# Twelve heads' softmax weights turned by VectorE and two DMAs in place of TensorE

## The chip, the cores and the metric

The kernel runs on one core of a Trainium2 chip. That core has a matrix engine (TensorE, PE in the profile; its weight loads are PEld), three engines for the rest (VectorE = DVE, ScalarE = ACT, GpSimd = POOL), a queue engine (SyncE = SP) and sixteen DMA engines that carry what any queue issues. The metric is the device time of one execution in microseconds (us), lower is better; times are given as the median of several runs.

## The reference

The reference is a two-layer encoder on 256 tokens of width 2048 in float32. A layer modulates and normalises `x`, projects it to the rows of two attention mixers and two gates, merges both mixers through their gates, projects back and adds; then a gated feed-forward part with a depthwise convolution follows. Mixer A has 8 heads over 2 groups of keys (a window of 128 tokens and a learned sink), mixer B has 8 heads over a 64-wide grid with a learned bias. For each head:

```python
s = jnp.einsum('bnqgrd,bnkgd->bgrnqk', qb, kw) * (HEAD_DIM ** -0.5)
p = jnp.exp(s - m)
p = p / (jnp.sum(p, axis=-1, keepdims=True) + jnp.exp(snk - m))
o = jnp.einsum('bgrnqk,bnkgd->bnqgrd', p, vw)
```

A head's `p` is a 256 x 256 matrix of softmax weights with queries in its rows. The product with the values sums over keys, so on this chip, which sums over partitions, `p` has to be turned first: keys into partitions.

## The kernel before

All large matrices come as one stream of weights per layer: units of 128 x 2048 float32 (1 MB), 232 to a layer, loaded by SP into four buffers `raw`. `unit_steps` (L280) makes two float32r halves of each half unit: ScalarE copies the upper part (L297) and VectorE subtracts it (L298), into four buffers `hl`. A half unit is named by its number here: 30.0 and 30.1 are the two halves of unit 30. TensorE takes three products from them (`feature_block`, L314 to L316, or `tokens`, L377 to L379). Modulation weights `aw` share the `raw` buffers and are reduced on VectorE (L226).

Small work runs beside that stream. After each unit `Paced.tick` (L258) first runs the functions that were deferred to this tick and then advances each job by its rate, in steps per unit. The attention of a layer is such a job (`attention`, L842): a step of the job advances every live head by one `yield` and starts at most one more. ATT gives the steps per unit while mixer A's rows arrive, ATT_B from the end of mixer A's projection on; what is left is run at once by `bg.finish(job)` (L952). In `attend` (L602) a head makes scores `sc` on TensorE (L607), masks and finds the maximum on VectorE (L610), takes exponentials and scales by the denominator on ScalarE (L618, L626), yields, turns `p` by four transposes on TensorE into the PSUM tile `tp` (L631), splits that into `pT` (L389 and L390, in `split`), yields, and multiplies with the values into `po` (L639), which becomes `oA` or `oB` (L641, L642).

The tile framework schedules each engine's queue from this program order, adds the waits, and each engine runs its own queue in order. SP issues all DMAs of this kernel. GpSimd does little here: among other things the power -0.5 for the norms of queries and keys (`rsqrt`, L441, tile `qrs`), for which VectorE then waits in `norm` (L556, tile `qn`). `packs` hold the rows of queries, keys and values; `qTa[:, i]` is head i's turned query in mixer A, `b[:, 8 + i]` and `b[:, i]` are query and key of a head in mixer B. In layer 1 (SCORES_3) a head first copies its query and key into float32r halves, so that those rows are free from then on.

Of the kernel before, what the change touches and what calls it, by code (L numbers as in the profile page):

```python
# [26 lines left out]
EPS = 1e-6  # L27
NEG = -1e30
SCALE = HEAD ** -0.5
GRID_W, NA_KH, NA_KW = 64, 8, 16  # L30


QKV_GROUPS = [1024, 0, 512, 2560, 3584, 1536, 3072, 4096, 2048]
# [44 lines left out]

H_RATE = [2.7, 1.7]

ATT = [1.288, 0.4]
ATT_B = [0.21, 0.21]

SCORES_3 = (1,)

ADA_ORDER = [[p * KC + k for k in range(KC) for p in ps] for ps in ((0, 1), (2,), (3, 4), (5,))]
ADA_ORDER = [i for part in ADA_ORDER for i in part]
# [47 lines left out]
def encoder(ctx: ExitStack, tc: tile.TileContext, a: dict, out: bass.AP):  # L135
# [16 lines left out]
    sm = pool("sm", 3)  # L152
    mm = pool("mm", 4, space=bass.MemoryType.PSUM)
    ax = pool("ax", 3, space=bass.MemoryType.PSUM)

    ident = const.tile([P, P], F32, name="ident")
    make_identity(nc, ident[:])
# [118 lines left out]
                pass  # L276

    bg = Paced()

    def unit_steps(l, u, by_halves=False):  # L280

        raw = rawp.tile([P, UB * P], F32, name=f"w{l}_{u}", tag="raw")
        if not by_halves:
            nc.sync.dma_start(raw[:], a["ws"][l, u])
        halves = []
        streamed = any(m == "w_in" and mo < GATE_A // P for m, _, mo in STREAMS[l][u * UB : (u + 1) * UB])
        at = OFF if streamed else 0
        for j in range(2):  # L290
            n = UB * P // 2
            hl = hlp.tile([P, 2 * n + ROW], F32R, name=f"hl{l}_{u}_{j}", tag="hl")
            hl = hl[:, at : at + 2 * n].rearrange("p (a n) -> p a n", a=2)
            r = raw[:, j * n : (j + 1) * n]
            if by_halves:
                nc.sync.dma_start(r, a["ws"][l, u][:, j * n : (j + 1) * n])
            nc.scalar.copy(hl[:, 0], r)  # L297
            nc.vector.tensor_tensor(out=hl[:, 1], in0=r, in1=hl[:, 0].bitcast(F32), op=ALU.subtract)  # L298
            halves.append(hl)
            if j == 0:  # L300
                yield halves
# [84 lines left out]
    def split(dst, src, scale=None):  # L386

        if scale is None:
            nc.scalar.copy(dst[:, 0], src)  # L389
            nc.vector.tensor_tensor(out=dst[:, 1], in0=src, in1=dst[:, 0].bitcast(F32), op=ALU.subtract)  # L390
            return
        nc.scalar.activation(out=dst[:, 0], in_=src, func=AF.Copy, scale=scale)
        nc.vector.scalar_tensor_tensor(
            out=dst[:, 1], in0=src, scalar=scale, in1=dst[:, 0].bitcast(F32), op0=ALU.mult, op1=ALU.subtract
        )
# [203 lines left out]

        return ((0, 0), (0, 1), (1, 0))[: 2 * len(x) - 1]  # L600

    def attend(q, k, v, p, mask, scale, sink, o):  # L602

        sc = ax.tile([P, 2, S], F32, name="sc", tag="ax")
        for t in range(2):
            for i, j in by(q):
                nc.tensor.matmul(sc[:, t], q[i][:, t * P : (t + 1) * P], k[j], start=i + j == 0, stop=(i, j) == by(q)[-1])  # L607
        m = sm.tile([P, 2], F32, name="m", tag="m")
        for t in range(2):
            nc.vector.tensor_tensor_reduce(  # L610
                out=p[:, t], in0=sc[:, t], in1=mask[:, t], scale=scale, scalar=-3.0e38 if sink is None else sink,
                op0=ALU.add, op1=ALU.max, accum_out=m[:, t : t + 1],
            )
        nm = sm.tile([P, 2], F32, name="nm", tag="nm")
        nc.vector.tensor_scalar(out=nm[:], in0=m[:], scalar1=-1.0, scalar2=None, op0=ALU.mult)
        den = sm.tile([P, 2], F32, name="den", tag="den")
        for t in range(2):
            nc.scalar.activation(out=p[:, t], in_=p[:, t], func=AF.Exp, bias=nm[:, t : t + 1], accum_out=den[:, t : t + 1])  # L618
        if sink is not None:
            es = sm.tile([P, 2], F32, name="es", tag="es")  # L620
            nc.scalar.activation(out=es[:], in_=nm[:], func=AF.Exp, bias=sink)
            nc.vector.tensor_tensor(out=den[:], in0=den[:], in1=es[:], op=ALU.add)
        ri = sm.tile([P, 2], F32, name="ri", tag="ri")
        nc.vector.reciprocal(out=ri[:], in_=den[:])
        for t in range(2):
            nc.scalar.activation(out=p[:, t], in_=p[:, t], func=AF.Copy, scale=ri[:, t : t + 1])  # L626
        yield
        tp = ax.tile([P, 2, S], F32, name="tp", tag="ax")
        for k in range(2):
            for t in range(2):  # L630
                nc.tensor.transpose(tp[:, k, t * P : (t + 1) * P], p[:, t, k * P : (k + 1) * P], ident[:])  # L631
        pT = at.tile([P, 2, 2, S], F32R, name="pT", tag="pT", bufs=1)
        split(pT, tp[:])
        v = v()
        yield
        po = ax.tile([P, 512], F32, name="po", tag="ax")
        for i, j in by(v):
            for b in range(2):
                nc.tensor.matmul(po[:, :S], v[i][:, b], pT[:, j, b], start=i + j + b == 0, stop=i + b == 2)  # L639
        o = o()  # L640
        nc.scalar.copy(o[:, 0], po[:, :S])  # L641
        nc.vector.tensor_tensor(out=o[:, 1], in0=po[:, :S], in1=o[:, 0].bitcast(F32), op=ALU.subtract)  # L642
# [115 lines left out]
    for l in range(L):  # L758
# [41 lines left out]
        def head_a(i):  # L800
            g = i // (HA // GA)
            if i >= 6:
                oA.append(paired(F32R, f"oA{l}_{i}"))
            elif i % 2 == 0:
                o = place(("y0", "y1", "y2")[i // 2], 4, F32R, f"oA{l}_{i}")
                oA.extend((o[:, :2], o[:, 2:]))
            q = in_halves(qTa[:, i], f"qA{l}_{i}", "qh", l in SCORES_3)
            if i % (HA // GA) == 0:
                kvs[0] = in_halves(kTa[:, g], f"kA{l}_{g}", "kh", l in SCORES_3)
            k = kvs[0]  # L810
            yield
            p = at.tile([P, 2, S], F32, name="p", tag="p")

            def v():
                if i % (HA // GA) == 0:
                    kvs[1] = in_halves(packs[0][:, 1:4:2, g * HEAD : (g + 1) * HEAD], f"vA{l}_{g}", "vh", True)
                return kvs[1]

            yield from attend(q, k, v, p, tables[0], SCALE, sink[:, i : i + 1], lambda: oA[i])

        def head_b(hb):
            b, i = packs[1 + hb // 4], hb % 4
            v = b[:, 4:8].rearrange("p (t a) s -> p t (a s)", t=2)
            p = at.tile([P, 2, S], F32, name="p", tag="p")
            nc.sync.dma_start(p[:], a["bias"][l, hb])
            q = in_halves(b[:, 8 + i], f"qB{l}_{hb}", "qh", l in SCORES_3)
            k = in_halves(b[:, i], f"kB{l}_{hb}", "kh", l in SCORES_3)
            yield
            yield from attend(
                q, k, lambda: in_halves(v[:, :, i * HEAD : (i + 1) * HEAD], f"vB{l}_{hb}", "vh", True), p, p, 1.0, None,  # L830
                lambda: oB_of(hb),
            )

        def oB_of(hb):
# [314 lines left out]
```

## Time and profile before

| What | us |
|---|---|
| Median of 3 runs | 2664.6 |
| Lowest and highest | 2664.26 and 2664.67 |
| Profiled execution: span from its first instruction to its last | 2663.2 |
| TensorE busy in it | 2650.9 |
| VectorE busy | 2102.2 |
| ScalarE busy | 1412.8 |
| GpSimd busy | 36.2 |

The page gives the profiled execution's time as its span; no other time of it is listed. The median of the runs stands 1.4 us above that span.

In the lines of the profile a group reads: source line, engine, operation, output tile <- input tiles, shapes, x count, then busy time, mean length in ns, and the idle time before with what ended it. A row of the timeline or of the chain of waits begins with its start and its length in us. A row of the view of waits reads: who waited, for whom, us in total, times, longest. A row of DMA issues ends with the KB of one and the median us from issue to landing.

### The profile page before, as it was taken

What the parts mean: (1) busy time and instruction counts of PE and PEld (TensorE: products, weight loads), DVE (VectorE), ACT (ScalarE), POOL (GpSimd) and SP (SyncE); (2) the same over time, 40 slices, a digit from 0 to 9 for tenths busy, and PEclk for the clock granted to TensorE, in tenths of its full rate; (3) what the DMA queues carried; (4) which work ended last, traced back from release to release, by engine and by line L of the source; (5) the groups of instructions that cost most, each with busy time, mean ns of one, the idle gap of its engine ahead of it and who ended that gap; (6) DMA issues with size and microseconds to landing.
All of it is one profiled execution on the core that took longest, in us unless ns stands there. A gap on an engine that the chain in (4) does not pass through costs nothing.

```text
span 2663.2 us, 50845 instructions
## 1 busy us (share of the span) xinstructions
PE 2650.9 (100%) x21256; PEld 2565.7 (96%) x21256; DVE 2102.2 (79%) x2959; ACT 1412.8 (53%) x2284; POOL 36.2 (1%) x25
## 2 busy tenths in 40 slices
PE   9999999999999999999999999999999999999999
PEld 7888899999999999999998889999999999999999
DVE  8898998997987888788976667768888866655664
ACT  5445865456644555355555566554565445544553
POOL 0001100000000000000000000000000000000000
PEclk9999999999999999999999999999999999999999
DMA  9987789885787878788766666666747765555554
GB/s 372 351 327 292 262 300 352 317 320 199 291 294 287 302 288 295 289 294 289 290 217 254 228 229 231 245 252 253 285 173 288 297 256 190 190 194 194 197 191 143
DMA packets 102039, 700.41 MB, mean 263 GB/s; under 512 B 12721, under 2 KB 15025, under 8 KB 17969
## 3 DMA queue, kind: packets, MB, share of 16 engines
q1 hardware_dynamic: 101810, 697.17, 71.4%
q8 instruction: 166, 2.72, 0.4%
q14 instruction: 63, 0.52, 0.1%
HBM read 695.03 MB, written 2.10 MB: 262 GB/s over the span
## 4 chain that ended last, share of the span: by engine, by line
PE 89%; DVE 6%; ACT 1%; issue 1%; DMA 1%; POOL 0%; SPq 0%; DVEq 0%; ACTq 0%
PE ps L314 25%; PE ps L316 25%; PE ps L315 25%; PE ps_t L377 4%; PE ps_t L379 4%; PE ps_t L378 4%; DVE hl L298 2%; DVE aw L226 2%; DMA aw<-in_aw 1%; PE sc L607 1%; PE po L639 1%; ACT hl L297 1%; PE tp L631 1%; POOL qrs L441 0%; PE qtp L580 0%
## 5 line engine op out<-in xcount | busy, mean ns | idle before, releaser
L298 DVE TENSOR_TENSOR hl<-w,hl 128x1024 fp32r<-128x1024 f32 x928 | 1128.3, 1222 | 360.0 <-ACT hl L297 357.6
L297 ACT CAST hl<-w 128x1024 fp32r<-128x1024 f32 x928 | 970.7, 1049 | 748.5 <-PE ps L316 518.1
L314 PE MATMUL ps<-h,hl 128*128 128x256 f32 x3328 | 922.8, 277 | 1.3 <-DVE ya L915 0.6
L315 PE MATMUL ps<-h,hl 128*128 128x256 f32 x3328 | 919.8, 276 | 0.0
L316 PE MATMUL ps<-h,hl 128*128 128x256 f32 x3328 | 919.8, 277 | 0.0
L314 PEld LDWEIGHTS ps<-h,hl 128*128 128x128 f32 x3328 | 624.8, 188 | 2.4 <-DVE ya L915 0.8
L315 PEld LDWEIGHTS ps<-h,hl 128*128 128x128 f32 x3328 | 625.3, 188 | 0.4 <-DVE h L470 0.2
L316 PEld LDWEIGHTS ps<-h,hl 128*128 128x128 f32 x3328 | 624.4, 188 | 0.0
L226 DVE CUSTOM_DVE_ANT_0 aw<-aw,cact,ab 128x2048 f32<-128x2048 f32 x189 | 443.5, 2347 | 48.8 <-DMA aw<-in_aw 47.8
L377 PE MATMUL ps_t<-hl,h 128*128 128x512 f32 x576 | 223.1, 392 | 2.6 <-ACT h L469 2.1
L378 PE MATMUL ps_t<-hl,h 128*128 128x512 f32 x576 | 224.9, 391 | 0.3
L379 PE MATMUL ps_t<-hl,h 128*128 128x512 f32 x576 | 224.3, 390 | 0.0
L994 DVE SCALAR_TENSOR_TENSOR u<-ps,cw,u 128x255 f32<-128x255 f32 x304 | 146.1, 481 | 66.5 <-ACT u L992 62.2
L992 ACT ACTIVATE u<-ps,cw 128x256 f32<-128x256 f32 x152 | 85.9, 565 | 187.9 <-PE ps L316 187.5
L316 PE MATMUL ps<-merged,hl 128*128 128x256 f32 x512 | 141.8, 277 | 0.4 <-DVE hl L298 0.4
L315 PE MATMUL ps<-merged,hl 128*128 128x256 f32 x512 | 141.6, 277 | 0.0
L314 PE MATMUL ps<-merged,hl 128*128 128x256 f32 x512 | 141.6, 277 | 0.0
L315 PE MATMUL ps<-act_o,hl 128*128 128x256 f32 x512 | 141.4, 276 | 0.0
L316 PE MATMUL ps<-act_o,hl 128*128 128x256 f32 x512 | 141.3, 276 | 0.0
L314 PE MATMUL ps<-act_o,hl 128*128 128x256 f32 x512 | 141.2, 276 | 0.0
L377 PEld LDWEIGHTS ps_t<-hl,h 128*128 128x128 f32 x576 | 107.9, 188 | 26.1 <-ACT h L469 3.1
L378 PEld LDWEIGHTS ps_t<-hl,h 128*128 128x128 f32 x576 | 108.1, 188 | 23.7 <-DVE hl L298 1.9
(231 smaller groups left out, 4612.5 us busy)
## 6 DMA issues: line engine op xcount, KB each, us to landing
w<-in_ws SPq DMA_DIRECT2D x463, 1024.0 KB, 4.9
aw<-in_aw SPq DMA_DIRECT2D x189, 1024.0 KB, 6.1
p<-in_bias SPq DMA_DIRECT2D x16, 256.0 KB, 4.2
x<-in_xT SPq DMA_DIRECT2D x4, 512.0 KB, 5.3
aw_o<-in_aw SPq DMA_DIRECT2D x2, 1024.0 KB, 12.3
out<-x SPq DMA_DIRECT2D x16, 128.0 KB, 2.1
w<-in_ws SPq DMA_DIRECT2D x2, 512.0 KB, 11.7
aw_b<-in_aw SPq DMA_DIRECT2D x1, 1024.0 KB, 18.1
```

The lines of the kernel that those rows point to most:

```text
L226: nc.vector.tensor_tensor_reduce(out=raw[:], in0=raw[:], in1=cact[:], scale=1.0, scalar=ab[:, i : i + 1], op0=ALU.mult, op1=ALU.add, accum ...
L297: nc.scalar.copy(hl[:, 0], r)
L298: nc.vector.tensor_tensor(out=hl[:, 1], in0=r, in1=hl[:, 0].bitcast(F32), op=ALU.subtract)
L314: nc.tensor.matmul(out, hi, act[0], start=first, stop=False)
L315: nc.tensor.matmul(ps[:, :S], hi, act[1], start=False, stop=False)
L316: nc.tensor.matmul(out, lo, act[0], start=False, stop=last)
L377: nc.tensor.matmul(ps[:], xh, hi, start=kc == kcs[0], stop=False)
L378: nc.tensor.matmul(ps[:], xh, lo, start=False, stop=False)
L379: nc.tensor.matmul(ps[:], xl, hi, start=False, stop=kc == kcs[-1])
L607: nc.tensor.matmul(sc[:, t], q[i][:, t * P : (t + 1) * P], k[j], start=i + j == 0, stop=(i, j) == by(q)[-1])
L992: nc.scalar.activation(out=u, in_=ps, func=AF.Identity, scale=w[:, 1:2], bias=w[:, 3:4])
L994: nc.vector.scalar_tensor_tensor(out=u[:, to], in0=ps[:, of], scalar=w[:, j : j + 1], in1=u[:, to], op0=ALU.mult, op1=ALU.add)
```

## The change

In layer 1 six heads of mixer A and six of mixer B (MOVED) no longer turn `p` on TensorE. VectorE transposes it in blocks of 32 x 32 into two rows that are free by then: for mixer A the head's own query row and a spare tile (two buffers, tag `r`), for mixer B the head's query and key rows. Eight DMAs on GpSimd's queue then write those blocks to their turned places in a DRAM tile `pY`, four for each row of blocks, each of 32 partitions in pieces of 32 elements (128 bytes). Two DMAs on SP's queue read the turned matrix back into the same two rows, and `pT` is split from there in two pieces of 128 x 256 in place of one of 128 x 512.

When the read-back is issued is fixed by `later`: three units (mixer A) or four (mixer B) after the head was turned, or when the head comes to need it. It carries a manual dependence on the last weight split on VectorE that had been made by then (`halved`). A moved head takes two more `yield`s. For layer 1 ATT goes from 0.4 to 0.42 and ATT_B from 0.21 to 0.32.

```diff
+BEHIND = mybir.DependencyInfo(mybir.DependencyClass.Sync, mybir.DependencyReason.DATA)
+BLOCK = 32
-ATT = [1.288, 0.4]
-ATT_B = [0.21, 0.21]
+ATT = [1.288, 0.42]
+ATT_B = [0.21, 0.32]
+BACK = [3, 4]
+MOVED = [(0, 0), (6, 6)]
...
+    dram = pool("dram", 2, space=bass.MemoryType.DRAM)
...
+    def later(n, fn):
+        if n == 0:
+            fn()
+        else:
+            bg.defer(lambda: later(n - 1, fn))
+
+    def turned_blocks(p, rows):
+        y = dram.tile([P, 2, S], F32, name="pY", tag="pY")
+        to = y[:].rearrange("(b i) k (t a j) -> t a i k b j", i=BLOCK, t=2, a=P // BLOCK)
+        for t, row in enumerate(rows):
+            nc.vector.transpose(out=row, in_=p[:, t])
+            src = row.rearrange("p (k b j) -> p k b j", k=2, j=BLOCK)
+            for a in range(P // BLOCK):
+                nc.gpsimd.dma_start(to[t, a], src[a * BLOCK : (a + 1) * BLOCK])
+        return y
...
-            nc.vector.tensor_tensor(out=hl[:, 1], in0=r, in1=hl[:, 0].bitcast(F32), op=ALU.subtract)
+            halved[0] = nc.vector.tensor_tensor(
+                out=hl[:, 1], in0=r, in1=hl[:, 0].bitcast(F32), op=ALU.subtract
+            ).ins.name
...
-    def attend(q, k, v, p, mask, scale, sink, o):
+    def attend(q, k, v, p, mask, scale, sink, o, rows=None):
...
+        if rows is not None:
+            rows = rows()
+            y = turned_blocks(p, rows)
+
+            def back():
+                for k in range(2):
+                    tc.add_manual_dep(nc.sync.dma_start(rows[k], y[:, k]).ins, halved[0], BEHIND)
+
+            back = once(back)
+            later(BACK[sink is None], back)
+            yield
+            yield
+            back()
+            pT = at.tile([P, 2, 2, S], F32R, name="pT", tag="pT", bufs=1)
+            for k in range(2):
+                split(pT[:, :, k], rows[k])
+        else:
+            tp = ax.tile([P, 2, S], F32, name="tp", tag="ax")
...
+            def rows():
+                spare = ev.tile([P, S], F32, name=f"spare{l}_{i}", tag="r", bufs=2)
+                return [qTa[:, i], spare[:]]
+
+            yield from attend(
+                q, k, v, p, tables[0], SCALE, sink[:, i : i + 1], lambda: oA[i], rows if i < MOVED[l][0] else None
+            )
...
-                lambda: oB_of(hb),
+                lambda: oB_of(hb), (lambda: [b[:, 8 + i], b[:, i]]) if hb < MOVED[l][1] else None,
```

`once` makes a function run one time only.

More of the change, by code (lines that the diff above doesn't have):

```diff
@@ L278, in encoder, with once, run @@
     bg = Paced()
+    halved = [None]
+    def once(fn):
+        due = [fn]
+        def run():
+            if due:
+                due.pop()()
+        return run
+    def later(n, fn):
[12 more added lines that the diff above has]
+        return y
     def unit_steps(l, u, by_halves=False):
@@ L627, in attend @@
         yield
[L628 to L633, printed above, removed]
+        if rows is not None:
[14 more added lines that the diff above has]
+            tp = ax.tile([P, 2, S], F32, name="tp", tag="ax")
+            for k in range(2):
+                for t in range(2):
+                    nc.tensor.transpose(tp[:, k, t * P : (t + 1) * P], p[:, t, k * P : (k + 1) * P], ident[:])
+            pT = at.tile([P, 2, 2, S], F32R, name="pT", tag="pT", bufs=1)
+            split(pT, tp[:])
         v = v()
@@ L817, in v @@
                 return kvs[1]
-            yield from attend(q, k, v, p, tables[0], SCALE, sink[:, i : i + 1], lambda: oA[i])
+            def rows():
[4 more added lines that the diff above has]
+            )
         def head_b(hb):
```

## The prediction

> **What bounds the kernel now.** I read the profile's page first (parts 1, 2 and 4), then the stretch of layer 1's attention.
>
> ```profile
> span 2663.2 us, 50845 instructions
> PE 2650.9 (100%) x21256; PEld 2565.7 (96%) x21256; DVE 2102.2 (79%) x2959; ACT 1412.8 (53%) x2284; POOL 36.2 (1%) x25
> PEclk9999999999999999999999999999999999999999
> PE 89%; DVE 6%; ACT 1%; issue 1%; DMA 1%; POOL 0%; SPq 0%; DVEq 0%; ACTq 0%
> ```
>
> TensorE is the bound: it lacks 2663.2 - 2650.9 = 12.3 us of being busy from end to end, its granted clock is in the top tenth in all slices, and the chain that ended last runs through it for 89%. Work taken from it, in a stage where it waits for nothing, comes off the span. The diff moves six heads of mixer A and six of B in layer 1, whose attention runs from about 1500 to 1810 us. The view of the stretch, and TensorE's own waits in it:
>
> ```profile
> 1500.00:1810.00 310.00, 309.64 (x2299) 292.59 (x2298) 214.67 (x347) 181.93 (x361) 4.91 (x3) 1.00 0.64 236
> PE ps L315 <- DVE oB L642: 0.3, 1, 0.3
> ```
>
> The columns are the stretch, its length, and the busy time of PE, PEld, DVE, ACT and POOL, then clock, DMA share and GB/s. TensorE misses 0.4 us in 310; VectorE has 310 - 214.7 = 95 us free, ScalarE 128, GpSimd 305, and the DMA engines 0.36 x 310 = 112 us.
>
> **What goes.** Each moved head loses four transposes (L631). The view by line gives their duration, the chain of waits of the stretch (start, length, what) their share of the path, the timeline their starts:
>
> ```profile
> L631 PE MATMUL tp<-ident,p 128*128 128x128 f32 x64 | 9.6, 273 | 0.1
> ...
> 1600.23 0.71 PE po L639 x6
> 1600.94 0.44 PE tp L631 x4
> 1601.37 0.69 PE sc L607 x6
> ...
> 1633.22 0.66 PE tp L631 x4
> ...
> 1766.73 0.44 PE tp L631 x4
> ...
> 1600.07 0.87 PE L639 MATMUL po<-pT,vA 128*128 128x256 f32 x6
> 1600.78 0.60 PE L631 MATMUL tp<-ident,p 128*128 128x128 f32 x4
> 1601.13 0.94 PE L607 MATMUL sc<-kA,qA 128*128 128x256 f32 x6
> 1601.90 0.40 PE L377 MATMUL ps_t<-hl,h 128*128 128x512 f32 x1
> ```
>
> One transpose lasts 273 ns, but they overlap: four of them hold the array from 1600.78 to 1601.13, 0.35 us, and the six score products behind them take 0.77 us to their successor where the six `po` products take 0.71. The chain charges 0.44 us to a group, and so it does in all but one of its groups in this stretch; I take 0.44. Twelve heads: 12 x 0.44 = 5.3 us (4.2 by the starts alone).
>
> [...]
>
> The end of the attention gains too. In the built order the last `po` group stood behind weight unit 75's second half and now stands behind the first half of unit 71, with the first product that needs it (unit 76) where it was: the rates ATT and ATT_B bring more turns than the two added `yield`s cost. So TensorE's 0.3 us wait for `oB` should go: 5.3 + 0.3 = 5.6 us.
>
> **What is added, and what hides it.** VectorE: two 32 x 32 block transposes of 128 x 256, and two splits of 128 x 256 for one of 128 x 512. ScalarE likewise copies in two pieces.
>
> ```profile
> L390 DVE TENSOR_TENSOR pT<-tp,pT 128x512 fp32r<-128x512 f32 x16 | 10.9, 682 | 0.1
> L390 DVE TENSOR_TENSOR qB<-packB,qB 128x256 fp32r<-128x256 f32 x8 | 3.4, 420 | 0.0
> L298 DVE TENSOR_TENSOR hl<-w,hl 128x1024 fp32r<-128x1024 f32 x102 | 124.1, 1223 | 74.8 <-ACT hl L297 74.4
> L297 ACT CAST hl<-w 128x1024 fp32r<-128x1024 f32 x101 | 105.7, 1048 | 82.2 <-PE ps L316 49.8 <-PE ps_t L379 32.4
> ```
>
> The splits cost 2 x 0.42 - 0.68 = 0.16 us a head. No block transpose is in the trace; by 256 columns it lies between the 0.42 of a split and, if it ran at half speed, 0.84; I take 0.42. That is 12 x (0.16 + 0.84) = 12 us of VectorE against 95 free. The cover is seen in the last two rows: ScalarE waited 82 us for TensorE to give back `hl` buffers, VectorE behind it, so the feed runs ahead. How far: 102 half units in 310 us are 3.0 us each with the attention between them, four `hl` buffers are some 12 us of TensorE's work, and a half needs 1.05 + 1.22 us to be made and up to 2.35 for a modulation product in front: about 8 us that ScalarE or VectorE may stand still before TensorE does.
>
> DMA: twelve heads write 256 KB and read it back, 6.3 MB beside 73 MB (236 GB/s x 310 us) that took 0.64 of the engines. At that rate it is 17 us of 112 free; pieces of 128 B may be dearer, and up to six times that fits.
>
> GpSimd's queue: eight issues a head, 96 in all, of 256 pieces each. The trace has no DMA from that queue. Bounds from the nearest rows (an issue on SP, GpSimd's own arithmetic on 8 columns with its waiter, and small transfers to their landing):
>
> ```profile
> L441 POOL TENSOR_TENSOR qrs<-qss,mhalf x3: 1637/1637/1639, 1534.6 to 1613.4; 128x8 f32<-128x8 f32 x3
> DVE qn L556 <- POOL qrs L441: 5.4, 3, 1.8
> 1539.90 0.33 SPq L225 DMA_DIRECT2D aw<-in_aw  x1
> out<-x SPq DMA_DIRECT2D x16, 128.0 KB, 2.1
> gains<-in_gains SPq DMA_DIRECT2D x2, 2.0 KB, 4.4
> ```
>
> Between 0.33 us (SP's issue) and 4.4 us (each landing awaited, which eight semaphores in turn don't ask for) I take the row of the same engine, 1.64, as the upper end of what is likely: 8 x 1.64 = 13 us a head, and 2.1 to land. What it has to meet is the read-back. In the built order head 0 is turned behind half 30.1 of the weights and its read-back on SP waits for half 32.1; these are (VectorE's timeline)
>
> ```profile
> 1515.33 1.23 DVE L298 TENSOR_TENSOR hl<-w,hl 128x1024 fp32r<-128x1024 f32 x1 [0.58 <-ACT hl L297]
> ...
> 1528.23 2.35 DVE L298 TENSOR_TENSOR hl<-w,hl 128x1024 fp32r<-128x1024 f32 x2
> ...
> 1537.52 2.35 DVE L298 TENSOR_TENSOR hl<-w,hl 128x1024 fp32r<-128x1024 f32 x2
> ```
>
> (unit 30's second half is 30.1.) 1515.33 + 1.23 and two turnings of 0.42 make 1517.4, and 32.1 ends at 1528.23 + 1.18 = 1529.4: 12 us. 13 + 2 us would hold SP back by 3 us, and behind it `w` of unit 35, then ScalarE's and VectorE's splits of the row, which stand half a unit later. That is inside the 8 us. The dependence on the split itself costs nothing: the next weight load waits for the same raw buffer (SP waited for VectorE anyway; below it three of its issues, ScalarE's first read of unit 35, and the landings):
>
> ```profile
> SPq L286 <- DVE hl L298: 65.2, 23, 5.5
> 1528.35 5.29 SPq L286 DMA_DIRECT2D w<-in_ws  x3
> 1541.04 1.05 ACT L297 CAST hl<-w 128x1024 fp32r<-128x1024 f32 x1 [2.34 <-PE ps_t L379]
> w<-in_ws SPq DMA_DIRECT2D x50, 1024.0 KB, 5.2
> ```
>
> Two more issues of 0.33 us a head on SP are 0.7 us in front of a load. Unit 35's is the first of three from 1528.35 and first read by ScalarE at 1541.04, 12.7 us for a landing of 5.2, so SP too may be 7 us late. Heads 1 to 5 follow each other by 2.6 units, 14 us, just over the 13 of the queue; the heads of B have three to four units before their read-back.
>
> The tightest place is `qrs`, GpSimd's roots for mixer B's rows. It now stands in that queue behind 17 issues (heads 0 and 1 and the first of head 2), and VectorE waits for it in `qn` right behind half 34.1, at 1537.5 + 2.35 = 1539.9. With s us an issue `qrs` ends at 1517.4 + 17 s + 1.64, and the 8 us are used up at 17 s = 28.9, s = 1.7. Below 1.7 I cost all of it at nothing; above, each 0.1 us is 1.7 us of TensorE.
>
> **Sum.** 5.6 us off TensorE, nothing back: the profiled execution's span goes from 2663.2 to 2657.6. The median of the runs shown is 2664.6, 1.4 above that span; I carry the difference over: 2659.0 us.
>
> **Rivals.**
> *Part of it comes back.* s lies between 1.6 and 2.1, or the read-backs land later than the 2.1 us of `out`, as the 4.4 of `gains` would have it, and SP, `qn` and the splits each pass their cover once or twice. For s = 2.1 `qrs` ends 37.3 us after 1517.4, 14.8 past 1539.9: 6.8 us beyond cover, 2659.0 + 6.8 = 2666; a typical value between is 2663. The two landing rows and the single tight place speak for it, against it that a gap of VectorE can be caught up in its 95 free us.
> *The queue becomes the bound (the other side).* At s = 2.5 six heads need 48 x 2.5 = 120 us. Head 0 is turned at 1517.4 and head 5's read-back follows its split, half 44.1, whose row is
>
> ```profile
> 1601.40 1.23 DVE L298 TENSOR_TENSOR hl<-w,hl 128x1024 fp32r<-128x1024 f32 x1 [1.55 <-ACT hl L297]
> ```
>
> at 1602.6: 85 us, and 11 more by SP's and `hl`'s cover. 26 us late in A, some of it again in B: 2659 + 26 = 2685. It decides from s = 2.2 on, where the loss passes 5.6 + 5.3. For it: no row shows s. [...]
> *The durations count.* Were a transpose worth its 273 ns, 48 x 0.273 = 13.1 us, 2651.5. The starts speak against it.
> *It shortens nothing.* If the feed set the pace, TensorE would wait elsewhere and the time stay at 2664.6. ScalarE's 82 us of waiting for TensorE speak against that.
>
> **Chances.** Forecast 0.55, partly back 0.20, queue 0.18, durations 0.02, nothing 0.05. A change of 0.2%, about what a measurement of this kernel can tell, is 5.3 us, 2659.3: the forecast lies on that line. Its own range is 2658.0 (nothing but the gain) to 2661.0 (4.2 us, and 0.6 back), and I give 0.35 of its 0.55 to below the line. Faster 0.35 + 0.02 = 0.37; same 0.20 + 0.17 of partly back + 0.05 = 0.42; slower 0.18 + 0.03 = 0.21. The range leaves out the durations and the worse half of the queue: 2657.8 to 2672.
>
> **What would show it.** Right: 64 - 48 = 16 transposes of `tp` left in layer 1, TensorE busy over 309 of 310 us there and the next stage starting 5 us earlier; 96 issues on POOL less than 1.7 us apart; `qn` waiting less than 8 us for `qrs`; the read-backs landed before ScalarE asks, or ScalarE's waits on them under 4 us. Wrong: TensorE waiting for `hl`, `w` issued later than its buffer came free because SP waited for GpSimd's DMAs, `qn` waiting over 8 us, or a DMA share near 1 in the stretch.

## The result, and the profile after

The changed kernel takes 2672.1 us against 2664.7 us, both medians of six runs: a ratio of 1.0029, 95% interval 1.0018 to 1.0041. It is slower by 0.29%. The forecast was 2659.0 us, and its range ended at 2672.0.

The profiled execution took 2669.4 us. First its page, parts 1 and 3, then the view of the stretch (length, busy time of PE, PEld, DVE, ACT and POOL, clock, DMA share, GB/s), then the lines of the transposes and the block turnings:

```profile
span 2667.7 us, 51058 instructions
PE 2650.6 (99%) x21208; PEld 2564.1 (96%) x21208; DVE 2108.6 (79%) x2995; ACT 1412.1 (53%) x2296; POOL 95.5 (4%) x121
...
q0 software_dynamic: 3072, 3.15, 0.4%
```

```profile
1500.00:1810.00 310.00, 304.24 (x2214) 285.66 (x2213) 217.72 (x374) 179.85 (x368) 64.85 (x99) 0.99 0.72 253
```

```profile
L685 PE MATMUL tp<-ident,p 128*128 128x128 f32 x16 | 3.0, 310 | 0.0
L309 DVE STREAM_TRANSPOSE packA<-p 128x256 f32<-128x256 f32 x6 | 2.6, 439 | 0.6 <-ACT p L663 0.6
```

The 48 transposes are gone from TensorE (64 before, 16 now), and a block turning costs VectorE 0.44 us. But TensorE, which missed 0.4 us of these 310 before, now misses 5.8. Its own waits between 1480 and 1830 us (total, times, longest):

```profile
PE ps_t L415 <- DVE hl L333: 3.8, 2, 2.4
PE po L693 <- DVE pT L427: 1.8, 1, 1.8
```

There are three gaps, near 1573, 1591 and 1632 us, all in the stretch of the A heads. The second is the longest. SP's waits between 1568 and 1580 us and its issues; VectorE's timeline; TensorE's rows at the gap:

```profile
SPq L671 <- DMA pY<-packA: 4.5, 1, 4.5
...
1578.09 0.33 SPq L671 DMA_DIRECT2D packA<-pY  x1
1578.52 0.38 SPq L671 DMA_DIRECT2D spare<-pY  x1
1579.00 0.38 SPq L321 DMA_DIRECT2D w<-in_ws  x1
1579.47 0.38 SPq L231 DMA_DIRECT2D aw<-in_aw  x1
```

```profile
1576.09 3.50 DVE L333 TENSOR_TENSOR hl<-w,hl 128x1024 fp32r<-128x1024 f32 x3 [0.46 <-ACT hl L332]
1586.69 2.35 DVE L232 CUSTOM_DVE_ANT_0 aw<-aw,cact,ab 128x2048 f32<-128x2048 f32 x1 [7.10 <-DMA aw<-in_aw]
...
1591.51 2.35 DVE L333 TENSOR_TENSOR hl<-w,hl 128x1024 fp32r<-128x1024 f32 x2
```

```profile
1589.95 0.39 PE L414 MATMUL ps_t<-hl,h 128*128 128x512 f32 x1
1592.78 0.80 PE L415 MATMUL ps_t<-hl,h 128*128 128x512 f32 x1 [2.44 <-DVE hl L333]
```

SP, which issues in order, stands 4.5 us at a read-back because GpSimd's writes of `pY` haven't landed. The weight load behind it goes out late, and the load of the modulation rows `aw` follows it by 0.47 us. The `aw` load itself is hardly late: it waited 0.2 us for its own buffer and goes out at 1579.47, in the kernel before at 1578.77. But it lands 7.1 us after its issue, where the eight `aw` loads between 1500 and 1650 us took 4.7 to 5.0 us before: it shares the DMA engines with that weight load, and their busy share is about 1 from 1581 to 1585 us (410 to 438 GB/s). VectorE, also in order, comes to the `aw` product with nothing loaded and stands 7.1 us (2.9 at the same product before); the split of the next weights is queued behind that product, and TensorE runs dry for 2.4 us.

Why the writes were late is seen on VectorE. A head's two turnings don't stand together there:

```profile
1557.22 0.44 DVE L309 STREAM_TRANSPOSE packA<-p 128x256 f32<-128x256 f32 x1
...
1568.60 0.42 DVE L427 TENSOR_TENSOR pT<-spare,pT 128x256 fp32r<-128x256 f32 x1
...
1569.34 0.44 DVE L309 STREAM_TRANSPOSE spare<-p 128x256 f32<-128x256 f32 x1
```

For heads 3, 4 and 5 the second turning comes 12.1, 15.2 and 5.0 us after the first, each time right behind the split of an earlier head that reads its `spare`, of which there are two. So four of the eight writes go out that much later; the last of head 3 is issued at 1573.36 and lands at 1578.01, and the read-back goes out at 1578.09. The run without transfers below has the same order (1552.87 and 1564.95 us for head 3). That the two buffers set this order is argued from the rows and the code; a third buffer was not tried.

At the third gap, too, an `aw` product waited in front of the splits of the weights and of `pT`:

```profile
1627.59 2.35 DVE L232 CUSTOM_DVE_ANT_0 aw<-aw,cact,ab 128x2048 f32<-128x2048 f32 x1 [1.61 <-DMA aw<-in_aw]
...
1632.13 0.68 DVE L427 TENSOR_TENSOR pT<-tp,pT 128x512 fp32r<-128x512 f32 x1
```

No read-back stands in front of this load: SP issued it at 1622.71 after 8.1 us of waiting for VectorE to free its buffer, which is as long as in the run without transfers, and it landed in 4.7 us. VectorE was late by then; what made it so is not followed further here.

Over the stretch VectorE's waits for `aw` grew from 7.4 to 24.0 us, and ScalarE's waits for `nm`, which VectorE makes, from 3.9 to 28.1:

```profile
DVE aw L226 <- DMA aw<-in_aw: 7.4, 6, 2.9
ACT p L618 <- DVE nm L615: 3.9, 4, 1.3
```

```profile
ACT p L655 <- DVE nm L652: 28.1, 12, 5.9
DVE aw L232 <- DMA aw<-in_aw: 24.0, 9, 7.1
DVE qn L593 <- POOL qrs L478: 7.1, 4, 1.9
```

(The first fence is of before, the second of after.) Each of the two longer gaps is then charged once more: the granted clock falls to half behind it. Four stretches of 3.41 us around the second gap (the clock stands third from the end):

```profile
1585.64:1589.05 3.41, 3.41 (x17) 2.82 (x16) 2.36 (x3) 0.12 (x1) 0.00 (x0) 1.00 0.06 24
1589.05:1592.46 3.41, 1.29 (x6) 0.75 (x4) 3.41 (x11) 0.83 (x3) 1.24 (x3) 1.00 0.64 209
1592.46:1595.88 3.41, 3.09 (x7) 2.48 (x8) 2.78 (x6) 1.99 (x6) 1.20 (x2) 0.50 0.96 281
1595.88:1599.29 3.41, 3.41 (x22) 3.02 (x21) 2.52 (x3) 3.41 (x7) 1.23 (x2) 1.00 0.55 187
```

The same stands behind the third gap (1633.42 to 1636.84 us). An account of this execution: 5.6 us gained, 5.6 us of waits, and two stretches at half clock, by estimate worth 3.41 / 2 = 1.7 us each, make +3.4; the span grew by 4.5 us, so that 1.1 us has no name here.

### The profile page after: what moved, and what is told of

It reads as the page before. It is cut to its first block, busy times and chain, and to the rows that moved or that the text cites. A ratio compares the mean times of both kernels' runs of the same rounds, so it can differ in the third digit from the quotient of the medians.

```text
span 2667.7 us, 51058 instructions
## 1 busy us (share of the span) xinstructions
PE 2650.6 (99%) x21208; PEld 2564.1 (96%) x21208; DVE 2108.6 (79%) x2995; ACT 1412.1 (53%) x2296; POOL 95.5 (4%) x121
## 3 DMA queue, kind: packets, MB, share of 16 engines
q1 hardware_dynamic: 105266, 700.32, 71.8%
## 4 chain that ended last, share of the span: by engine, by line
PE 91%; DVE 4%; ACT 2%; issue 1%; DMA 1%; POOL 0%; DVEq 0%; POOLq 0%; ACTq 0%
PE ps L351 26%; PE ps L353 26%; PE ps L352 26%; PE ps_t L415 3%; PE ps_t L416 3%; PE ps_t L414 3%; DVE hl L333 2%; DVE aw L232 1%; ACT hl L332 1%; PE sc L644 1%; DMA aw<-in_aw 1%; PE po L693 1%; POOL qrs L478 0%; PE tp L685 0%; ACT qsq L584 0%
```

## Experiments

Two explanations stood against each other at first, with a third beside them. SP held: SP waits at the read-back, and the loads behind it come late. Traffic: the added transfers themselves make landings late. Order: the turnings, the two-piece splits and the later steps alone eat the lead of the weight splits. Medians below are set against the kernel before on the same chip. Each ratio has an interval of about 0.1% to either side, so a difference of two runs is good to some 3 to 4 us.

**No transfers (no_dma).**

```diff
-            for a in range(P // BLOCK):
-                nc.gpsimd.dma_start(to[t, a], src[a * BLOCK : (a + 1) * BLOCK])
...
-                    tc.add_manual_dep(nc.sync.dma_start(rows[k], y[:, k]).ins, halved[0], BEHIND)
+                    pass
```

> VectorE's twelve block-wise turnings, the two-piece splits and the later steps stay; GpSimd's 96 writes and SP's 24 read-backs are left out, so the softmax weights of these twelve heads are turned only within their 32x32 blocks. The kernel after takes 2672 us, the kernel before 2664.7. SP-held theory (SP waits at a read-back for GpSimd's writes, and the weight and ada loads behind it come late and bunched): no read-back, so the forecast sum of the prediction comes out, about 2659 us. Traffic theory (the added transfers themselves make landings late): also about 2659 us. Order theory (the new order on VectorE and ScalarE, with ScalarE waiting for nm, alone eats the lead of the weight splits): 2668 to 2672 us, with the gaps on TensorE near 1572, 1590 and 1631 us still there.

Measured 2659.6 us against 2664.8; ratio 0.9979 (0.9971 to 0.9988). The forecast comes out within a microsecond. Order by itself costs no time, so it falls as the cause; it does shorten the lead of some splits, as the last part shows. The stretch:

```profile
1500.00:1810.00 310.00, 309.81 (x2302) 292.66 (x2300) 228.08 (x390) 186.56 (x377) 4.92 (x3) 1.00 0.66 242
```

**The writes alone (write_only).** Only the second half of that edit.

> GpSimd's 96 writes stay, SP's 24 read-backs are left out (the weights of the twelve heads stay turned within their blocks only). SP-held theory: SP waits for nothing new, about 2659 us, ada waits of VectorE back near 7 us in all. Traffic theory: the writes are most of the added packets (24,576 pieces of 128 B), so most of the loss stays, 2666 to 2671 us. Order theory: 2668 to 2672 us.

Measured 2664.9 us, ratio 1.0000 (0.9991 to 1.0009): 5.3 us come back, where SP-held expected nothing. It is not the traffic that the trace shows, though, but a third thing, GpSimd's queue. VectorE's, TensorE's and GpSimd's timelines:

```profile
1543.77 0.69 DVE L593 TENSOR_TENSOR qn<-ps_t,qrs 128x512 f32<-128x512 f32 x1 [6.60 <-POOL qrs L478]
```

```profile
1545.65 0.50 PE L415 MATMUL ps_t<-hl,h 128*128 128x512 f32 x1 [0.86 <-DVE hl L333]
```

```profile
1540.80 0.62 POOL L312 DMA_DIRECT2D pY<-spare  x1 [0.85 <-issue]
1541.45 0.61 POOL L312 DMA_DIRECT2D pY<-packA  x1
1542.07 1.67 POOL L478 TENSOR_TENSOR qrs<-qss,mhalf 128x8 f32<-128x8 f32 x1
```

The roots `qrs` were due when VectorE had `qss`, at 1536.7 us, and stand behind 17 writes until 1542.1; VectorE waits 6.6 us in `qn`. TensorE has gaps at 1545 and 1574 us.

**The read-backs alone (read_only).** The writes are left out and the read-back takes `a["xT"][:, k]` in place of `y[:, k]`.

> GpSimd's 96 writes are left out; SP's 24 read-backs stay at their places, with their dependence on a weight split, but take 128 KB each from the input x (so the twelve heads use other numbers as weights). SP-held theory: SP waits only for the split (8 us in five waits in the kernel after) and no longer for pY (31 us in eighteen), so most of the loss goes: 2659 to 2663 us. Traffic theory: the 3.1 MB read back remain next to the weight loads, 2662 to 2668 us. Order theory: 2668 to 2672 us.

Measured 2662.2 us, ratio 0.9990 (0.9981 to 0.9999): 2.6 us above the run without transfers, within what SP-held named and at the edge of traffic. The profiled execution is the longest of its eleven (2667.9 us): one `aw` wait of 6.4 us is left there, and TensorE idles 0.6 and 1.8 us.

**The read-back on GpSimd's queue (pool_read).**

```diff
-                    tc.add_manual_dep(nc.sync.dma_start(rows[k], y[:, k]).ins, halved[0], BEHIND)
+                    tc.add_manual_dep(nc.gpsimd.dma_start(rows[k], y[:, k]).ins, halved[0], BEHIND)
```

> All is computed and moved as in the kernel after, but the 24 read-backs are issued on GpSimd's own queue, behind its writes, with the same dependence; SP holds only weights, ada rows and biases. SP-held theory: SP is free, so 2659 to 2663 us, unless the read-back then comes later than ScalarE's split asks for it. Traffic theory: the same bytes move, 2668 to 2673 us. Order theory: 2668 to 2673 us.

Measured 2677.3 us, ratio 1.0044 (1.0032 to 1.0057), worse than either number. SP is free, but ScalarE now waits for the read-back itself:

```profile
ACT pT L426 <- DMA packB<-pY: 7.6, 1, 7.6
ACT pT L426 <- DMA packA<-pY: 7.6, 1, 7.6
```

This speaks for neither explanation; the read-back was moved to another queue and came later still.

**All transfers, but SP waits for none of GpSimd's (both_free).**

```diff
-            src = row.rearrange("p (k b j) -> p k b j", k=2, j=BLOCK)
+            src = tables[0][:, t].rearrange("p (k b j) -> p k b j", k=2, j=BLOCK)
...
-                    tc.add_manual_dep(nc.sync.dma_start(rows[k], y[:, k]).ins, halved[0], BEHIND)
+                    tc.add_manual_dep(nc.sync.dma_start(rows[k], a["xT"][:, k]).ins, halved[0], BEHIND)
```

> All 96 writes of GpSimd and all 24 read-backs of SP stay in their places, but the writes take their numbers from the constant mask (issued after the same turnings) and the read-backs take theirs from the input x, so a read-back waits for its weight split alone and for no write (the twelve heads use other numbers as weights). Measured so far: 2659.6 without any of the transfers, +5.3 us with the writes alone, +2.6 us with the reads alone, 2672 with all. SP-held theory: the two prices add, 2659.6 + 5.3 + 2.6 = 2667.5 us, and the 4.6 us left to 2672 are SP's waits for pY. Traffic theory (writes and reads disturb each other whether SP waits or not): 2670 to 2673 us.

Measured 2662.7 us against 2665.3, ratio 0.9992 (0.9983 to 1.0001). That is 4.8 us less than the sum of the two prices, and far from the traffic's 2670. The same bytes as in the change, without the wait, cost some 3 us in place of 12.5; the interval reaches from nothing to 6. Here `qrs` came as late as with the writes alone, at 1543.8 us, but `qn` waited 5.0 us in place of 6.6, and TensorE missed 0.4 us of the stretch between 1480 and 1830 us in place of 3.2.

**Which heads (b_only, a_only, b8).** `MOVED` for layer 1 becomes (0, 6), (6, 0) and (0, 8).

> Only the six heads of the second kind (B) are moved, the six of the first kind (A) are turned on TensorE as before. In the trace of the kernel after every wait of TensorE lies among the A heads, none among the B heads. If the loss belongs to the A stretch alone, the B heads keep their gain: 6 x 0.44 = 2.6 us and 0.3 us of the end wait, 2664.7 - 2.9 = 2661.8 us. If the transfers as such cost, wherever they lie: half of the loss stays, 2665 to 2668 us.

Measured 2662.0 us against 2665.3, ratio 0.9988 (0.9979 to 0.9996).

> Only the six A heads are moved. If the loss belongs to the A stretch: 2672 + 2.6 = 2674 to 2675 us. If the transfers as such cost, wherever they lie: half of it goes, 2667 to 2669 us.

Measured 2673.8 us, ratio 1.0032 (1.0019 to 1.0045).

> All eight B heads are moved and no A head. If the loss belongs to the A stretch: 8 x 0.44 + 0.3 = 3.8 us, 2660.9 us, faster than both kernels. The last two heads have fewer steps behind them, and if their read-back comes late at the end of attention it is 2662 to 2665 us. If the transfers as such cost: 2666 to 2670 us.

Measured 2660.8 us, ratio 0.9986 (0.9977 to 0.9995). All three fall within 0.3 us of the first theory's numbers: the loss belongs to the A heads, and the B heads keep their gain. Moving the eight B heads and no other is the best complete kernel measured here, 4.5 us faster than before.

**The read-back one unit later (back45).** `BACK = [4, 5]` in place of `[3, 4]`.

> The whole computation; only the place of the read-back changes: four weight units after the turning for A heads and five for B heads, instead of three and four (about 5.5 us later each), with ScalarE's split at its old place. In the kernel after SP waits 31 us in eighteen read-backs for pY, 4.9 us at most, so that one unit more ends nearly all of these waits. SP-held theory: 2664 to 2668 us if ScalarE then waits for the read-back itself, 2660 to 2664 if it doesn't. Traffic theory: 2670 to 2673 us, as after. Rival: the split stays where it was, the read-back lands behind it, and ScalarE's waits for packA and packB grow from 5 us to over 20 us, 2675 us or more.

Measured 2666.6 us against 2665.2, ratio 1.0007 (0.9998 to 1.0016). Six of the 7.4 us lost go with one number. That is still 2.6 us above what SP-held named for this case, in which ScalarE hardly waits for the read-back (0.5 us). SP's waits for `pY` fall from 31.0 to 7.5 us and VectorE's for `aw` to 11.0. But the first gap on TensorE is now the queue's (the stretch, VectorE's and TensorE's timelines, and GpSimd's in front of `qrs`):

```profile
1500.00:1810.00 310.00, 304.61 (x2240) 286.43 (x2239) 220.97 (x377) 181.79 (x370) 63.97 (x99) 1.00 0.72 255
```

```profile
1537.80 0.24 DVE L477 TENSOR_SCALAR qss<-qss 128x8 f32<-128x8 f32 x1
1546.43 0.69 DVE L593 TENSOR_TENSOR qn<-ps_t,qrs 128x512 f32<-128x512 f32 x1 [8.38 <-POOL qrs L478]
1548.31 0.50 PE L415 MATMUL ps_t<-hl,h 128*128 128x512 f32 x1 [2.61 <-DVE hl L333]
```

```profile
1539.45 0.61 POOL L312 DMA_DIRECT2D pY<-spare  x1 [1.38 <-issue]
1543.46 0.62 POOL L312 DMA_DIRECT2D pY<-spare  x1 [3.39 <-issue]
1544.10 0.61 POOL L312 DMA_DIRECT2D pY<-packA  x1
1544.73 1.66 POOL L478 TENSOR_TENSOR qrs<-qss,mhalf 128x8 f32<-128x8 f32 x1
```

In the kernel after this wait was hidden: the sums `qss` that the roots need came only at 1539.80 us there, 2.0 later than here, and `qn` waited no longer than before. So TensorE misses 5.4 us of the stretch here and 5.8 in the kernel after: the gaps were exchanged for others, at 1548 and 1579 us, of nearly the same sum. What differs between these two profiled executions (2666.6 and 2669.4 us) is the clock: 1.00 over this stretch against 0.99, no fall to half against two, 3.4 us by the estimate above.

**Later still, with more steps (late3, late4).** `BACK = [4, 5]` with three `yield`s before the split, and `[6, 7]` with four.

> The whole computation; read-backs four and five weight units after the turning, and ScalarE's split one step of the head later (three steps instead of two), so that neither SP nor ScalarE waits for pY. SP-held theory: what the run without waits for the writes gave, 2662 to 2664 us. Traffic theory: 2670 to 2673 us. Rival: the third step keeps each head open longer and shifts the order of VectorE and ScalarE, 2664 to 2668 us.

Measured 2673.6 us, ratio 1.0031 (1.0019 to 1.0042).

> As the run before it in this batch, with read-backs six and seven units after the turning and four steps before the split. SP-held theory: no further gain once SP waits for no pY, 2661 to 2664 us. Traffic theory: 2670 to 2673 us. Rival: the buffers of a head are held longer than the next heads need them, 2665 us or more.

Measured 2679.6 us, ratio 1.0054 (1.0041 to 1.0066). In these two runs the longer chain of steps lets A head 6 (in the second also 7), which is not moved, reach its values before head 4 has set those of their group, so it uses the other group's; the amount of work is the same. They decide nothing: in the first, SP waited up to 8.2 us for `pY` again and `qn` up to 8.0 for the roots, so the waits that they were to end were still there.

**Without A head 0 (skip0, skip0_back45, skip0_write, skip0_b8_back45).**

```diff
-                q, k, v, p, tables[0], SCALE, sink[:, i : i + 1], lambda: oA[i], rows if i < MOVED[l][0] else None
+                q, k, v, p, tables[0], SCALE, sink[:, i : i + 1], lambda: oA[i], rows if i < MOVED[l][0] and i else None
```

> The whole computation; as the kernel after, but A head 0 is turned on TensorE as before, so that eleven heads are moved and the roots qrs near 1536 us stand behind 9 of GpSimd's writes instead of 17. SP still waits for pY at its read-backs. Both-causes theory (SP's waits and the roots behind the writes): the qn wait is 1.8 us again, the waits for pY stay, 2664 to 2669 us. SP-held theory alone: 2670 to 2672 us less the waits of head 0's read-back, 2668 to 2671 us. Queue theory alone: 2660 to 2662 us.

Measured 2672.7 us against 2665.5, ratio 1.0024 (1.0015 to 1.0033).

> Eleven heads moved (without A head 0), and the read-back one weight unit later. The run with twelve heads and the later read-back gave 2666.6 us, with its first gap on TensorE where qn waited 8.4 us for qrs. Both-causes theory: neither the roots nor SP are late, so the time is that without transfers, 2659.6 + 0.4 = 2660.0, plus at most 2 us of traffic: 2660 to 2662.5 us. If something else (traffic, order) makes the rest of the loss: 2664 to 2667 us.

Measured 2664.6 us, ratio 0.9998 (0.9989 to 1.0007).

> GpSimd's writes of eleven heads (without A head 0) and no read-backs, so that the weights of these heads are turned within their blocks only. With twelve heads it was 2664.9 us, with qn waiting 6.6 us for qrs. Queue theory: the price of the writes is that wait, 2660 to 2661 us. Traffic theory: eleven twelfths of the 5.3 us stay, 2664 to 2665 us.

Measured 2663.6 us, ratio 0.9989 (0.9980 to 0.9998).

> The whole computation; five A heads (1 to 5) and all eight B heads moved, read-backs one weight unit later. Both-causes theory: one head more than before the change's twelve and no lasting wait, 2659 to 2661.5 us, below both kernels and at or below the 2660.8 us of the eight B heads alone. Else 2663 to 2666 us.

Measured 2663.0 us, ratio 0.9990 (0.9981 to 0.9999). All four miss what two causes gave: the first lies above every range named for it, the third between its two ranges, and the second and fourth in the range of something else. In the first two the edit moved the collision instead of ending it. GpSimd in the first:

```profile
1565.39 1.22 POOL L312 DMA_DIRECT2D pY<-spare  x2
1570.35 1.22 POOL L312 DMA_DIRECT2D pY<-spare  x2 [3.74 <-issue]
1571.59 1.67 POOL L478 TENSOR_TENSOR qrs<-qss,mhalf 128x8 f32<-128x8 f32 x1
```

The sums for these roots were there at 1567.3 us. The next group's roots now stand behind the writes of head 3, `qn` waits 6.0 us, and TensorE stands 4.5 us from 1572 us on; in the second run `qn` waits 6.2 us and TensorE 4.1 at the same place. That doesn't explain the third: without head 0 the writes alone leave TensorE idle for 0.4 us between 1480 and 1830 us, against 3.2 with it, as the queue theory has it, and what keeps its median 3 us above that theory lies outside the attention or in the spread of the executions (2660.3 to 2667.9 us). The fourth misses 1.6 us there.

**The roots out of GpSimd's queue (after_qv, back45_qv, write_qv).** In the change, in the later read-back and in the writes alone:

```diff
-        nc.gpsimd.tensor_tensor(out=dst, in0=src, in1=mhalf[:, :k], op=ALU.pow)
+        nc.vector.tensor_scalar(out=dst, in0=src, scalar1=0.0, scalar2=1.0, op0=ALU.mult, op1=ALU.add)
```

> As the kernel after, but the roots qrs of the query and key rows no longer stand in GpSimd's queue: VectorE fills qrs with ones in their place (the normalisation of these rows by their root mean square is left out). SP still waits for pY. SP-held theory (in the kernel after, SP's waits are what costs): nearly as after, 2669 to 2672 us. Queue theory (the roots behind the writes cost as much): 2664 to 2667 us.

Measured 2670.6 us against 2665.4, ratio 1.0018 (1.0009 to 1.0027), in the range of SP-held alone. TensorE misses 7.1 us of the 310.

> The later read-back (four and five units) and qrs filled on VectorE as in the run before it in this batch. With the roots on GpSimd the later read-back gave 2666.6 us. Both-causes theory: neither SP nor the roots are late, 2660 to 2663 us. If the traffic or the order makes the rest: 2665 to 2667 us.

Measured 2663.2 us, ratio 0.9990 (0.9982 to 0.9999), 0.2 us above the range of two causes. Its stretch in the profiled execution:

```profile
1500.00:1810.00 310.00, 309.82 (x2295) 292.55 (x2294) 227.71 (x393) 186.73 (x376) 58.87 (x96) 1.00 0.73 260
```

> GpSimd's 96 writes, no read-backs (the twelve heads' weights are turned within their blocks only), and qrs filled with ones on VectorE. With the roots on GpSimd the writes cost 5.3 us. Queue theory: they cost nothing now, 2659 to 2661 us. Traffic theory: 2663 to 2665 us.

Measured 2660.9 us, ratio 0.9982 (0.9973 to 0.9991), as the queue theory had it. Together with the earlier runs this is a table of two causes (median less that of before on the same chip, us):

| | read-back as in the change | one unit later | no read-back | no transfers |
|---|---|---|---|---|
| roots on GpSimd | +7.4 | +1.4 | +0.2 | -5.2 |
| roots off its queue | +5.2 | -2.1 | -4.4 | not run |

Along the first row SP's wait is worth 6.0 us, along the second 7.3. The second is the cleaner reading: in its profiled executions TensorE's missing time in the stretch goes from 7.1 to 0.2 us. The roots behind the writes are worth 2.2 (not resolved by itself), 3.5 and 4.6 us; that they count more the less SP hides them fits the traces, but the three numbers are too close to show it. The run without transfers misses 0.2 us of the stretch, so taking the roots off the queue has hardly anything to gain there. The difference of -4.4 and -5.2, which would be the writes as traffic, is less than can be resolved. So two waits of in-order queues make the loss: SP at the read-back first, GpSimd's roots behind its own writes second.

## Why the prediction was wrong, by its steps

*The gain: right.* It gave 5.6 us for 48 transposes at 0.44 and the end wait. Without the transfers the kernel is 0.21% faster, 5.6 us (3.2 to 7.7 by the interval). Counting the 273 ns durations would have given 13.

*The added compute: right in time, but it took cover.* A block turning takes 0.44 us where 0.42 was taken, and the run without transfers shows that all of it lies beside TensorE's work. What the sum didn't count is that the new order on VectorE leaves less lead in front of some weight splits (below).

*The pace of GpSimd's queue: right in size by luck, wrong in what it does.* The issues of the kernel after (duration least, median and most in ns; first and last start):

```profile
L312 POOL DMA_DIRECT2D pY<-packA x24: 612/615/782, 1517.3 to 1600.0; - x24
```

```profile
1517.33 2.00 POOL L312 DMA_DIRECT2D pY<-packA  x3 [25.43 <-DVE spare L309]
...
1540.28 0.61 POOL L312 DMA_DIRECT2D pY<-packA  x1 [1.29 <-DVE qss L477]
```

The first and the seventeenth issue stand 22.95 us apart, 1.43 us an issue (0.61 of it busy), below the 1.64 taken as the upper end and below the threshold of 1.7. With the writes alone it is 1.53, with the later read-back 1.64. The 1.64 came from a row of arithmetic, which has nothing to do with this pace; the landings of the writes fit it, a third of their median 4.3 us being 1.43 (last part). Still the roots cost 4.6 us where the writes ran alone, since the threshold rested on a later step.

*"Two turnings of 0.42 make 1517.4": right for head 0 alone.* For heads 3 to 5 the second turning, and with it half of the writes, comes 5 to 15 us after the first. Eight issues from one place, 13 us a head, did not hold for them, and SP waited 31.0 us in eighteen read-backs.

*"About 8 us that ScalarE or VectorE may stand still before TensorE does": this step failed.* It was a mean over 102 half units, made of buffers and durations (and its terms, 12 - 1.05 - 1.22 - 2.35, give 7.4). The two `qn` waits above measure it at 34.1, the place that the prediction called the tightest: 6.60 us of wait left TensorE idle for 0.86, and 8.38 us for 2.61, so 5.7 to 5.8 us were covered there. The lead has to be taken half unit by half unit, as the time from the end of VectorE's split to the first product of that half (products counted in order; the product behind it, 0.23 us later, is the first that reads VectorE's part). In the trace of before it is 4 to 9 us at most places, but 2.3 us for unit 41's second half and 2.5 for 47's:

```profile
1588.36 2.35 DVE L298 TENSOR_TENSOR hl<-w,hl 128x1024 fp32r<-128x1024 f32 x2
...
1591.90 0.39 PE L377 MATMUL ps_t<-hl,h 128*128 128x512 f32 x1
```

The first of these two splits ends at 1589.6, the product starts at 1591.9. In the run without transfers, where TensorE waits for nothing, the lead is 4.0 us for unit 34's second half (6.4 before), 1.7 for unit 39's first (5.0 before) and 2.4 for unit 41's second, and 4 to 8 for most others. The gaps at weight splits lie at these places: after at 39 and 41, the writes alone and the later read-back at 34 and 39, the reads alone at 39 and 41. In all of them a modulation product, a head's VectorE work or a wait stands between two weight splits. For unit 41 this could be read from the trace of before; the places at 34 and 39 became tight by the change's own order.

*"SP too may be 7 us late": wrong load.* That lead was read from a weight load. The load without lead is `aw`: VectorE waited for it in the kernel before already, up to 2.9 us. Behind a wait of 4.5 us on SP, 2.9 at the same product became 7.1. Of the 4.2 more, 2.4 are the landing of `aw` beside the late weight load (7.1 us after the issue, 4.7 before), 0.7 its issue, and 1.1 VectorE's coming earlier.

*"A gap of VectorE can be caught up in its 95 free us": wrong in place.* The free time lies between the tight places, and the next one comes a few units on.

*The clock: not foreseen.* Two of the three gaps were followed by half clock, some 3.4 us in the profiled execution by the estimate above.

*The rivals.* "Part of it comes back" named the right mechanism, read-backs late and SP, `qn` and the splits passing their cover, at 0.20; its 2663 to 2666 was too small, for it used the 8 us and full clock. The 0.21 given to "slower" came from the other rival. "The queue becomes the bound" gave the right side for a reason that is not there: no issue pace near 2.2. Of the signs listed, the 16 transposes left, the issues under 1.7 us apart (in the mean of the first 17), `qn` under 8 us and ScalarE's waits for read-backs under 4 us (3.4 at most) came true, so that they alone would have called the forecast right. TensorE's wait for `hl`, its 304.2 us of 310 and SP's waits for GpSimd's DMAs told otherwise. (A slip beside this: the range's lower end, 2658.0 for "nothing but the gain", should be 2659.0 by the sum.)

*What stays open.* The traffic as such lies between nothing and some 3 us (the run without SP's wait for writes, and the later read-back without the roots). Landings did come later beside it: of the `aw` loads between 1500 and 1650 us two took 7.1 and 7.5 us in the kernel after, where 5.0 was the most before. But with the writes alone and the roots off the queue VectorE waited at most 3.1 us for `aw` (2.9 before), and TensorE misses only 0.2 us of the 310 there, so that nothing of it came through. The runs with more steps were not explained further. That the spread of the kernel after (2669.4 to 2678.5 us) comes from how many of its gaps are followed by half clock was not tried.

## What to carry to other kernels

Give cover place by place, and in the order that the change will make: for each piece that the bound engine reads, the time between its making and its first use, and take the smallest near the change, not the mean. A read-back behind another engine's writes put the wait for them into the issuing queue here, 31.0 us of SP in eighteen read-backs, so list what stands behind it there and ask which of these loads had no lead; one weight unit more of distance was worth 6 us here. Ask also whether a transfer's parts are ready together: half of a head's writes waited for a second turning. And on a queue that also computes, ask what stands behind a burst of writes: with the writes alone the roots, 1.67 us of work, were due at 1536.7 us and started at 1542.07, behind 17 writes of 32 KB.

## What the runs showed of the hardware that was not expected

A gap of some 2 us in TensorE's work cost nearly as much again, by the estimate of 1.7 us for a stretch at half clock. The granted clock fell to 0.50 twice in the attention of the kernel after, at 1592.46 and at 1633.42 us, for 3.413 us each time. The two starts lie 40.96 us apart, 12 times 3.413. From the start of one product to the start of the next TensorE's three gaps are 1.75 us (from 1572.34), 2.83 (from 1589.95) and 2.06 (from 1630.82). The 3.41 us in front of the first fall, in which TensorE was busy for 1.29 us, stand in the section on the result. The same cut in steps of 3.41 us at the first gap with what follows it, and at the third with its fall:

```profile
1571.98:1575.40 3.41, 2.05 (x10) 1.37 (x9) 3.41 (x7) 2.03 (x4) 0.70 (x2) 1.00 0.58 161
1575.40:1578.81 3.41, 3.41 (x17) 2.83 (x16) 2.95 (x5) 2.57 (x3) 1.72 (x3) 1.00 0.62 231
...
1630.01:1633.42 3.41, 1.64 (x14) 1.44 (x13) 3.14 (x4) 0.00 (x0) 0.00 (x0) 1.00 0.71 242
1633.42:1636.84 3.41, 3.41 (x18) 3.41 (x17) 2.09 (x8) 1.83 (x6) 0.00 (x0) 0.50 0.98 397
```

So 1.29 and 1.64 us of work in such a step were followed by half clock, and 2.05 us were not. The length of a gap alone does not tell the cost here: the run with the later read-back has two gaps of 3.0 us with 0.39 us of TensorE's work in each, and no fall in the stretch (its clock is 1.00 over the 310 us).

```profile
1545.30:1548.30 3.00, 0.39 (x2) 0.00 (x0) 1.87 (x3) 1.04 (x1) 2.92 (x4) 1.00 0.19 29
1575.84:1578.82 2.98, 0.39 (x3) 0.00 (x1) 2.98 (x6) 1.71 (x5) 0.96 (x2) 1.00 0.99 347
```

What decides whether a gap is followed by half clock was not shown.

In the kernel after GpSimd's writes of 256 pieces of 128 B go out in bursts, with a median of 0.61 us for an issue, and between bursts the queue stands up to 4.6 us with no wait that the profile names:

```profile
POOL pY L312 <- issue: 71.8, 37, 4.6
```

That idle time, 71.8 us over 96 issues, is more than their 59 us of work. The landings in the trace fit it: none of the 96 writes goes out sooner than 0.31 us after the landing of the third write before it, and at no time are more than three between issue and landing. The first three land at 1523.66, 1523.82 and 1523.99 us, and the fourth goes out at 1523.97. Of the 50 writes that go out after a pause, 38 follow that landing by less than 0.45 us. The times from issue to landing:

```profile
DMA to landing us min/median/max: 1.9/4.3/7.2
```

A third of the median 4.3 us is 1.43 us, and the first seventeen issues stand 1.43 us apart. That the landings set this pace is an estimate from these numbers; no run changed them to show it, and how the pace goes with what else the DMA engines carry was not measured.
